# Channel weights of the first norm applied behind the transposes, in a one-core decoder layer

## The chip, the core and the metric

The kernel runs on one core of a Trainium2 chip. A core has a matrix engine (TensorE, PE in the profile), a vector engine (VectorE, DVE), a scalar engine (ScalarE, ACT), a small general engine (GpSimd, POOL), and queues from which transfers are started (SyncE, SP, carries nearly all of them here). The engines run on their own and wait for one another through semaphores. The metric is device time in microseconds (us) of one launch; lower is better.

## What is computed

One layer of a decoder trunk in float32: a norm, one wide input projection, three groups of heads (spatial gating, a gated delta rule, attention into 256 memory tokens), an output projection and a last norm. The change concerns the first norm and the norm of the memory tokens, each with a weight for every one of 2048 channels:

```python
def rmsnorm(x, g):
    xf = x.astype(jnp.float32)
    y = xf * lax.rsqrt(jnp.mean(xf * xf, axis=-1, keepdims=True) + EPS)
    return (y * g.astype(jnp.float32)).astype(x.dtype)

h = rmsnorm(x, ln_g[l])                      # x: 1024 x 2048
proj = h @ w_in[l]
...
m = rmsnorm(mem, mem_norm_g[l])              # mem: 256 x 2048
mk, mv = jnp.split(m @ w_mem_kv[l], 2, axis=-1)
```

## The kernel before

**Precision.** A float32 operand that has to be multiplied exactly enough is split into a high and a low part of the fast matmul type. `split_to` (L422) does this: ACT copies the source to the high part, DVE subtracts the high part from the source to get the low part. `triple` then issues three matmuls: high by high, high by low, low by high.

**Order.** Every instruction is recorded into a `Plan`. `Plan.issue` (L222) plays the recorded operations through a cost table (`price`, L181) and a priority (`rank`), engine by engine, and writes out the order that this gives. So all engines run a fixed program order that a planner chose when the kernel was built; a change of an operation's engine or of a buffer changes the order everywhere behind it. L277 is the one place from which all operations are issued, so every row of the profile has that line, and rows are told apart by their tiles.

**The first stage** (about the first 100 us) has three strands, which the planner interleaves:

- *Key and value weights.* The memory tokens are transposed and split (`spread_mem`, L521; tiles `gt` and `inv`). For each of 16 blocks `k` of 128 channels, `load_kv(k)` (L483) loads 128x1024 weights into a raw tile; ACT and DVE scale them by a column of the memory norm's weights (`gcol`, one column for each `k`) while splitting them into `whi` and `wlo`; PE accumulates 12 matmuls of 256 columns (keys, tiles `acc`) and 6 of 512 columns (values, the first two `dn` tiles). The raw tiles are a ring of four: two of `wraw`, two of `ut`. `kvmark` notes the last matmul of each `k`; some loads wait for such a mark.
- *The first norm's weights.* Each quarter of `ln_g` is loaded as one row into a `zg` tile. `spread_gain` (L532) spreads it over 128 partitions with a matmul against a row of ones, and ACT copies the result back. The four spread tiles are `gb`.
- *Tokens of x.* `prep(tt)` (L537) takes 128 tokens: sums of squares on ACT, a scale for each token from DVE and POOL, then for each quarter of the channels a DVE operation that multiplies by the token's scale and by `gb`, four PE transposes into a free bank (`spare()` hands out the last two `dn` banks in turn), and a hand-over `put`. For the first 512 tokens `put0` copies the bank to a `tn` tile on ACT, splits it into `ahi` and `alo`, and stores `tn` to `h0d`. For the other 512 tokens `prep1` runs later, beside the first projections, and `keep_rows` copies the bank to `tn` on ACT and stores it to `hTd`.

Behind the key and value matmuls PE starts on the projections: `project_first` (L871) goes over the first 256 tokens for all channels, then over the second 256. A quarter of channels of those tokens must be in `ahi` and `alo` before the matmuls on it. The weights of the projection come through the `wraw`, `whi` and `wlo` tiles in pieces of 512 columns of a row each (four blocks of 128 channels). In between come small preparations: a 105-row transpose of other weights (`y`), weights of the decay (`abw`), and weights of the spatial gating (tile `E`, transposed by PE, masked by DVE into `wsT`).

Of the kernel before, what the change touches and what calls it, by code (L numbers as in the profile page):

```python
# [12 lines left out]
ALU = mybir.AluOpType  # L13
# [4 lines left out]
P = 128  # L18
D = 2048
KT = D // P  # L20
NQ = 4
SEQ = 1024
HT = 512
# [39 lines left out]
class Plan:  # L63
# [21 lines left out]
    @contextmanager  # L85
    def rank(self, cls):
        old, self.cls = self.cls, cls
        yield
        self.cls = old
# [191 lines left out]
def kernel(  # L281
# [21 lines left out]
    x, mem, w_in, out = x[0], mem[0], w_in[0], out[0]  # L303
    w_mem_kv, w_out, conv_w = w_mem_kv[0], w_out[0], conv_w[0]
# [6 lines left out]
    V, S, G, PE, Q = R.dve, R.act, R.pool, R.pe, R.sp  # L311
    rank, behind = R.rank, R.behind

    def C(shape, name, dt=F32):
        return sb.tile(list(shape), dt, name=name, tag=name)[:]
# [38 lines left out]
    def bc(ap, n):  # L354
        return ap.unsqueeze(ap.ndim).to_broadcast(list(ap.shape) + [n])
# [4 lines left out]
    def tok(ap):  # L360

        return ap.rearrange("p (t c) -> p t c", c=P)
# [12 lines left out]
    kvraw = [*wraw.bufs]  # L375
# [5 lines left out]
    ring = {t: Slots(t, 4, [P, HT]) for t in ("kT", "qT", "vs", "kd", "ai")}  # L381
# [3 lines left out]
    zgb = ring["zg"].bufs  # L385
# [23 lines left out]
    ident, ones, utri = (C([P, P], n) for n in ("ident", "ones", "utri"))  # L409
# [12 lines left out]
    def split_to(hi, lo, src, eng):  # L422
        S.copy(hi, src)
        eng.tensor_tensor(out=lo, in0=src, in1=hi, op=ALU.subtract)
# [20 lines left out]
    def triple(a, l, r, start, stop, cls=9):  # L445

        mm(a, l[0], r[0], start, False, cls)
        mm(a, l[0], r[1], False, False, cls)
        return mm(a, l[1], r[0], False, stop, cls)
# [4 lines left out]
    def row_scale(xq):  # L454

        s = small()
        for c in range(4):
            S.activation(jk, xq[c], AF.Square, accum_out=s[:, c : c + 1])
        V.tensor_reduce(s[:, 4:5], s[:, 0:4], axis=AX.X, op=ALU.add)
        V.tensor_scalar(s[:, 4:5], s[:, 4:5], 1.0 / D, EPS, op0=ALU.mult, op1=ALU.add)  # L460
        rsqrt_to(s[:, 5:6], s[:, 4:5])
        return s[:, 5:6]


    def row_tiles(tag):
        if tag in ("inv", "gt", "ut"):
            return [b[:, i * HT : (i + 1) * HT] for b in (ring[tag](), ring[tag]()) for i in range(2)]
        return [ring[tag]() for _ in range(4)]

    gb = [ring["zg"]() for _ in range(4)]  # L470
    kvraw += [ring["ut"]() for _ in range(2)]
    mem_rows = [row_tiles("kT"), row_tiles("qT")]
    x_rows = {}

    def load_mem(q):
        for mt in range(2):
            Q.dma_start(mem_rows[mt][q], mem[mt * P : (mt + 1) * P, q * HT : (q + 1) * HT])

    def kv_parts(k):
        n = XW if k == 0 else 2 * XW  # L480
        return [slice(i, i + n) for i in range(0, 2 * XW, n)]

    def load_kv(k):  # L483
        for sl in kv_parts(k):
            Q.dma_start(kvraw[k % 4][:, sl], w_mem_kv[k * P : (k + 1) * P, sl])

    def load_x(tt, tag, after=(None,) * 4):
        x_rows[tt] = row_tiles(tag)
# [3 lines left out]

    y1 = C([P, 2 * NT, 32], "y1")
    rows = y1.rearrange("p c m -> p (c m)")[:, 0:P]
    mrow = rows[0:16]
    with rank(2):
        load_mem(0)
        S.dma_start(mrow, mem_norm_g[0].rearrange("(c p) -> c p", p=P))
        for c in range(4):
            S.dma_start(gb[c][0:1], ln_g[0:1, c * HT : (c + 1) * HT])  # L500
        for k in range(4):
            load_kv(k)
            if k == 1:
                load_mem(1)
    with rank(3):
        load_mem(2)
        load_mem(3)

    va, ka = dnr.bufs[0:2], acc
# [2 lines left out]
    def spare():  # L512
        turn["dn"] = 1 - turn["dn"]
        return flip[turn["dn"]]

    pt = spare()
    PE.transpose(pt[:, 0:16], mrow, ident[0:16, 0:16])
    gcol = C([P, 16], "gcol")
    with rank(1):
        V.tensor_copy(gcol, pt[:, 0:16])  # L520
    def spread_mem(q):  # L521
        h, l = (ring[t](F32R).rearrange("p (k n) -> p k n", k=4) for t in ("gt", "inv"))
        for mt in range(2):
            tp = spare()
            for k in range(4):
                PE.transpose(tp[:, k * P : (k + 1) * P], mem_rows[mt][q][:, k * P : (k + 1) * P], ident)
            sl = slice(mt * P, (mt + 1) * P)
            with rank(2):
                split_to(h[:, :, sl], l[:, :, sl], tok(tp), V)
        return h, l  # L530

    def spread_gain(c, pt):  # L532
        PE.matmul(pt, ones[0:1], gb[c][0:1], start=True, stop=True)
        with rank(3):
            S.copy(gb[c], pt)

    def prep(tt, put, bank):  # L537

        xq = x_rows[tt]
        r = row_scale(xq)  # L540
        for q in range(NQ):
            V.scalar_tensor_tensor(xq[q], xq[q], r, gb[q], op0=ALU.mult, op1=ALU.mult)
            tp = bank()
            for k in range(4):
                PE.transpose(tp[:, k * P : (k + 1) * P], xq[q][:, k * P : (k + 1) * P], ident)
            put(q, tok(tp))

    def keep_rows(dst, q, tt, tp):
        t = ring["tn"]()
        S.copy(t, tp.rearrange("p t c -> p (t c)"))  # L550
        Q.dma_start(dst[4 * q : 4 * q + 4, :, tt * P : (tt + 1) * P].rearrange("k p n -> p k n"), tok(t))

    def put0(tt):
        def put(q, tp):
            t = tok(ring["tn"]())
            with rank(1):
                S.copy(t, tp)
            with rank(2):
                split_to(ahq[q][:, tt], alq[q][:, tt], t, V)
            with rank(6):  # L560
                Q.dma_start(h0_d[4 * q : 4 * q + 4, :, tt * P : (tt + 1) * P].rearrange("k p n -> p k n"), t)

        return put
# [5 lines left out]
    mhl.append(spread_mem(1))  # L569
    for k in range(KT):  # L570
        mh, ml = mhl[k // 4]
        if k >= 4:
            with rank(3):
                load_kv(k)
        hi, lo = kvhi[k % 2], kvlo[k % 2]
        with rank(2):
            for sl in kv_parts(k):
                raw = kvraw[k % 4][:, sl]
                S.activation(hi[:, sl], raw, AF.Copy, scale=gcol[:, k : k + 1])
                V.scalar_tensor_tensor(lo[:, sl], raw, gcol[:, k : k + 1], hi[:, sl], op0=ALU.mult, op1=ALU.subtract)  # L580
        kk = k % 4
        for h in range(NX):
            sl = slice(h * P, (h + 1) * P)
            triple(ka[h][:, :NMEM], (hi[:, sl], lo[:, sl]), (mh[:, kk], ml[:, kk]), k == 0, k == KT - 1)
        for mt in range(2):
            sl = slice(mt * P, (mt + 1) * P)
            triple(va[mt], (mh[:, kk, sl], ml[:, kk, sl]), (hi[:, XW:], lo[:, XW:]), k == 0, k == KT - 1)
        kvmark.append(R.ops[-1])
        if 1 < k < 6:
            spread_gain(k - 2, spare())  # L590
        if k in (3, 7):
            mhl.append(spread_mem(k // 4 + 2))
        if k == 1:
            load_x(0, "vs", kvmark[1:2] * 4)
        if k == 4:
            load_x(1, "kd", kvmark[4:5] * 4)
        if k == 5:
            prep(0, put0(0), spare)
            for mt in range(2):
                rm.append(C([P, 1], f"rm{mt}"))  # L600
                V.tensor_copy(rm[mt], row_scale(mem_rows[mt]))
        if k == 7:

            dg, rmb = (ring["E"]()[:, 0:NMEM] for _ in range(2))
            for mt in range(2):
                V.tensor_scalar(dg[:, mt * P : (mt + 1) * P], ident, rm[mt], None, op0=ALU.mult)
            pt = spare()
            PE.matmul(pt[:, 0:NMEM], ones, dg, start=True, stop=True)
            S.copy(rmb, pt[:, 0:NMEM])
        if k == 9:  # L610
            prep(1, put0(1), spare)
            load_x(2, "kT", (kvmark[6], kvmark[7], kvmark[7], kvmark[8]))
        if k == 13:
            load_x(3, "qT", (kvmark[10], kvmark[11], kvmark[11], kvmark[12]))
            with rank(2):
                prep(2, put0(2), spare)
# [6 lines left out]
    for mt in range(2):  # L623
        t = [ring["ai"](F32R) for _ in range(2)]
# [9 lines left out]
    for h in range(NX):  # L634
        t = ring["vs"](F32R).rearrange("p (s m) -> p s m", s=2)
# [18 lines left out]
    pt = dnr()  # L654
# [30 lines left out]
    tp = dnr()  # L685
# [4 lines left out]
    tp = dnr()  # L690
    for g in range(NG):
        sl = slice(g * P, (g + 1) * P)
# [53 lines left out]
    def prep1(i):  # L746
        load_x(NT + i, "ut")
        prep(NT + i, lambda q, tp: keep_rows(hT_d, q, i, tp), over(scan_banks))
# [496 lines left out]
    ut = levels(state[2], *state[-1])  # L1245
# [313 lines left out]
    with rank(2.6):  # L1559
        for hf in range(2):  # L1560
            for p in range(NJ // 2, NJ):
                state = front_late(p, hf, late_inv[hf * 2 + p - NJ // 2])
                ut = levels(state[2], *state[-1])
# [38 lines left out]
    for n, (tag, to) in enumerate((("gt", mkT), ("inv", mv))):  # L1602
        for i in range(NX // 2):
            t = ring[tag](F32R).rearrange("p (h s m) -> p h s m", h=2, s=2)
# [190 lines left out]
```

## Time and profile before

| | us |
|---|---|
| device time, median of three runs | 1631.83 |
| lowest and highest of the three | 1628.95, 1632.06 |
| profiled execution, first to last instruction | 1631.6 |
| PE busy | 1613.6 (99%) |
| DVE busy | 1319.3 (81%) |
| ACT busy | 1025.9 (63%) |
| POOL busy | 114.7 (7%) |

The profiled execution has no other time than its span. A group row of the profile names the engine, the operation, the tile written and the tiles read, the shapes, the count, the busy time in us, the mean of one in ns, and then the idle time of the engine before such instructions. A timeline row gives start and duration in us and, in brackets, idle time before it and what ended that. A window row gives its stretch, its length, and the busy time of PE, PE's weight loads, DVE, ACT and POOL with their counts, then the granted PE clock, the DMA share and GB/s. Matmuls overlap in the records: a 512-column one is shown as 0.39 us, while the next starts 0.23 us after it.

### The profile page before, as it was taken

How to read it: one execution, taken by the hardware profiler on the slowest of the kernel's cores; microseconds unless marked ns; L12 is line 12 of the kernel's file. 1: busy time of each engine (PE TensorE's matmuls, PEld its weight loads, DVE VectorE, ACT ScalarE, POOL GpSimd, SP SyncE). 2: the span in 40 equal slices, each digit the busy share in tenths (PEclk: the TensorE clock that was granted, in tenths of full speed). 3: DMA queues.
4: the chain of work that ended last, by engine and by line, in shares of the span. 5: the costliest groups of instructions: out<-in, count | busy, mean ns of one | idle time of the engine just before them, and what ended most of it. 6: DMA issues, size and time to landing. Idle time of an engine off the chain costs nothing.

```text
span 1631.6 us, 25647 instructions
## 1 busy us (share of the span) xinstructions
PE 1613.6 (99%) x8570; PEld 1354.7 (83%) x8570; DVE 1319.3 (81%) x2288; ACT 1025.9 (63%) x2235; POOL 114.7 (7%) x139
## 2 busy tenths in 40 slices
PE   8999999999999999999999999999999999999997
PEld 6888888888888888888888888888888888888886
DVE  4876786858879869899999998888778897678875
ACT  5958674676755356877686547766657774344355
POOL 0100110020210000100101001001000000000001
PEclk9999999999999999999999999999999999999999
DMA  7888896886886867589867967889768889678646
GB/s 247 248 256 268 262 307 179 264 264 204 284 297 212 278 207 236 186 288 342 285 223 257 344 214 232 283 279 305 261 216 283 272 291 332 202 270 301 213 147 240
DMA packets 316846, 419.44 MB, mean 257 GB/s; under 512 B 51821, under 2 KB 140582, under 8 KB 316714
## 3 DMA queue, kind: packets, MB, share of 16 engines
q1 hardware_dynamic: 315010, 414.65, 77.8%
q0 software_dynamic: 1088, 2.10, 0.5%
q8 instruction: 67, 1.10, 0.3%
q10 hardware_dynamic: 616, 1.07, 0.2%
q14 instruction: 65, 0.53, 0.1%
HBM read 334.33 MB, written 82.87 MB: 256 GB/s over the span
## 4 chain that ended last, share of the span: by engine, by line
PE 95%; DMA 2%; DVE 2%; issue 1%; ACT 0%; POOL 0%; POOLq 0%; SPq 0%; DVEq 0%; ACTq 0%
PE acc L277 73%; PE dn L277 22%; DMA raws<-sd 1%; DMA kT<-in_mem_dram 1%; DVE wlo L277 1%; DVE alo L277 0%; DMA el<-vd 0%; DMA late<-kd 0%; DMA wraw<-in_w_in_dram 0%; DVE kT L277 0%; DVE kd L277 0%; ACT whi L277 0%; POOL small L277 0%; ACT jk L277 0%; DVE xr L277 0%
## 5 line engine op out<-in xcount | busy, mean ns | idle before, releaser
L277 PE MATMUL acc<-ahi,whi 128*128 128x512 f32 (+1 forms) x1152 | 451.4, 392 | 0.6 <-ACT whi L277 0.5
L277 PE MATMUL acc<-alo,whi 128*128 128x512 f32 (+1 forms) x1152 | 450.7, 392 | 0.0
L277 PE MATMUL acc<-ahi,wlo 128*128 128x512 f32 (+1 forms) x1152 | 450.0, 391 | 0.4 <-DVE wlo L277 0.4
L277 PEld LDWEIGHTS acc<-ahi,whi 128*128 128x128 f32 x1152 | 216.8, 188 | 42.0 <-ACT whi L277 1.0
L277 PEld LDWEIGHTS acc<-ahi,wlo 128*128 128x128 f32 x1152 | 216.8, 188 | 41.4 <-DVE wlo L277 0.6
L277 PEld LDWEIGHTS acc<-alo,whi 128*128 128x128 f32 x1152 | 216.9, 188 | 40.2
L277 PE MATMUL acc<-ahi,zh 128*128 128x512 f32 x736 | 233.6, 394 | 0.0
L277 ACT CAST whi<-wraw 128x512 fp32r<-128x512 f32 (+1 forms) x170 | 137.0, 807 | 102.3 <-PE acc L277 69.0
L277 ACT CAST ahi<-raws 128x1024 fp32r<-128x1024 f32 x131 | 137.4, 1049 | 84.0 <-PE acc L277 37.5
L277 DVE TENSOR_TENSOR alo<-raws,ahi 128x1024 fp32r<-128x1024 f32 x131 | 160.2, 1223 | 36.6 <-ACT ahi L277 36.0
L277 DVE TENSOR_TENSOR wlo<-wraw,whi 128x1024 fp32r<-128x1024 f32 (+1 forms) x138 | 134.5, 975 | 38.8 <-ACT whi L277 32.0
L277 PEld LDWEIGHTS acc<-ahi,zh 128*128 128x128 f32 x736 | 137.6, 188 | 27.1
L277 PE MATMUL acc<-ahi,zl 128*128 128x512 f32 x368 | 145.1, 394 | 0.0
L277 DVE TENSOR_TENSOR ahi<-y,ahi 128x1024 fp32r<-128x1024 f32 x65 | 79.3, 1220 | 21.3 <-ACT ahi L277 20.9
L277 ACT CAST ahi<-y 128x1024 fp32r<-128x1024 f32 x65 | 68.1, 1048 | 40.9 <-PE acc L277 23.0
L277 PEld LDWEIGHTS acc<-ahi,zl 128*128 128x128 f32 x368 | 69.3, 188 | 13.0
L277 ACT CAST zh<-wraw 128x1024 fp32r<-128x1024 f32 x36 | 37.8, 1049 | 43.8 <-PE acc L277 26.5
L277 POOL TENSOR_TENSOR hs<-hs,mhalf 128x4 f32<-128x4 f32 x32 | 48.0, 1502 | 234.3 <-DVE hs L277 223.8
L277 PE MATMUL dn<-whi,alo 128*128 128x512 f32 x152 | 59.0, 389 | 0.0
L277 PE MATMUL dn<-wlo,ahi 128*128 128x512 f32 x152 | 59.0, 389 | 0.0
L277 PE MATMUL dn<-whi,ahi 128*128 128x512 f32 x152 | 58.9, 389 | 0.0
L277 POOL TENSOR_TENSOR small<-small,mhalf 128x1 f32<-128x1 f32 x26 | 17.5, 677 | 581.5 <-DVE small L277 575.3
(408 smaller groups left out, 3210.4 us busy)
## 6 DMA issues: line engine op xcount, KB each, us to landing
wraw<-in_w_in_dram SPq DMA_DIRECT2D x86, 512.0 KB
raws<-sd SPq DMA_DIRECT2D x74, 512.0 KB
wraw<-in_w_in_dram SPq DMA_DIRECT2D x96, 256.0 KB
y<-in_w_in_dram SPq DMA_DIRECT2D x42, 512.0 KB
y<-sd SPq DMA_DIRECT2D x38, 512.0 KB
wraw<-in_w_out_dram SPq DMA_DIRECT2D x32, 512.0 KB
raws<-h0d SPq DMA_DIRECT2D x27, 512.0 KB
low<-wlo SPq DMA_DIRECT2D x32, 256.0 KB
```

Source lines behind the costliest of these rows:

```text
L277: o.fn(*o.args, **o.kw)
```

## The change

The rows of `ln_g` are no longer spread. They are loaded as 16 more rows beside those of the memory norm, and the one small transpose that makes `gcol` makes 32 columns instead of 16; `lcol` names the 16 new ones, four for each quarter. `prep` multiplies by the token's scale alone (`tensor_scalar` in place of `scalar_tensor_tensor`). Behind the transposes the channels lie on the partitions, and the copy from the bank to `tn`, which was ACT's, becomes a DVE multiplication by the column. This holds for `put0` and for `keep_rows`. `spread_gain`, its four matmuls and four ACT copies are gone. The two double tiles of `zg`, which `gb` held, join the ring of raw key and value weights: six instead of four, and the loads for `k` = 4 and 5 are issued between the third and the fourth quarter of the memory tokens.

```diff
-    gb = [ring["zg"]() for _ in range(4)]
-    kvraw += [ring["ut"]() for _ in range(2)]
+    kvraw += [ring["ut"]() for _ in range(2)] + zgb
+    NR = len(kvraw)
...
-            Q.dma_start(kvraw[k % 4][:, sl], w_mem_kv[k * P : (k + 1) * P, sl])
+            Q.dma_start(kvraw[k % NR][:, sl], w_mem_kv[k * P : (k + 1) * P, sl])
...
-    mrow = rows[0:16]
+    mrow = rows[0:32]
...
-        S.dma_start(mrow, mem_norm_g[0].rearrange("(c p) -> c p", p=P))
-        for c in range(4):
-            S.dma_start(gb[c][0:1], ln_g[0:1, c * HT : (c + 1) * HT])
+        S.dma_start(mrow[0:16], mem_norm_g[0].rearrange("(c p) -> c p", p=P))
+        S.dma_start(mrow[16:32], ln_g[0].rearrange("(c p) -> c p", p=P))
...
         load_mem(2)
+        for k in range(4, NR):
+            load_kv(k)
         load_mem(3)
...
-    PE.transpose(pt[:, 0:16], mrow, ident[0:16, 0:16])
-    gcol = C([P, 16], "gcol")
+    PE.transpose(pt[:, 0:32], mrow, ident[0:32, 0:32])
+    gcol = C([P, 32], "gcol")
...
+    lcol = [gcol[:, 16 + 4 * q : 20 + 4 * q] for q in range(NQ)]
...
-    def spread_gain(c, pt):
-        PE.matmul(pt, ones[0:1], gb[c][0:1], start=True, stop=True)
-        with rank(3):
-            S.copy(gb[c], pt)
...
-            V.scalar_tensor_tensor(xq[q], xq[q], r, gb[q], op0=ALU.mult, op1=ALU.mult)
+            V.tensor_scalar(xq[q], xq[q], r, None, op0=ALU.mult)
...
     def keep_rows(dst, q, tt, tp):
         t = ring["tn"]()
-        S.copy(t, tp.rearrange("p t c -> p (t c)"))
+        V.tensor_tensor(out=tok(t), in0=tp, in1=bc(lcol[q], P), op=ALU.mult)
...
             with rank(1):
-                S.copy(t, tp)
+                V.tensor_tensor(out=t, in0=tp, in1=bc(lcol[q], P), op=ALU.mult)
...
-        if k >= 4:
+        if k >= NR:
...
-                raw = kvraw[k % 4][:, sl]
+                raw = kvraw[k % NR][:, sl]
...
-        if 1 < k < 6:
-            spread_gain(k - 2, spare())
```

More of the change, by code (lines that the diff above doesn't have):

```diff
@@ L516 @@
     pt = spare()
-    PE.transpose(pt[:, 0:16], mrow, ident[0:16, 0:16])
-    gcol = C([P, 16], "gcol")
+    PE.transpose(pt[:, 0:32], mrow, ident[0:32, 0:32])
+    gcol = C([P, 32], "gcol")
     with rank(1):
-        V.tensor_copy(gcol, pt[:, 0:16])
+        V.tensor_copy(gcol, pt[:, 0:32])
+    lcol = [gcol[:, 16 + 4 * q : 20 + 4 * q] for q in range(NQ)]
     def spread_mem(q):
```

## Prediction

> **What bounds the kernel now.** I read the page first, for the engine that sets the end, then windows, to see where that engine has any idle time, then the timeline of PE and DVE in the stage that the change touches.
>
> ```profile
> span 1631.6 us, 25647 instructions
> PE 1613.6 (99%) x8570; PEld 1354.7 (83%) x8570; DVE 1319.3 (81%) x2288; ACT 1025.9 (63%) x2235; POOL 114.7 (7%) x139
> PE 95%; DMA 2%; DVE 2%; issue 1%; ACT 0%; POOL 0%; POOLq 0%; SPq 0%; DVEq 0%; ACTq 0%
> ```
>
> PE is busy 99% and makes 95% of the chain that ended last. Work taken from PE shortens the end one for one; work moved among ACT, DVE and DMA costs nothing until PE waits for it. In the windows the first figure behind the length is PE, the third DVE, the fourth ACT.
>
> ```profile
> 65.00:71.60 6.60, 6.42 (x44) 5.43 (x43) 6.60 (x12) 6.60 (x16) 0.23 (x1) 1.00 0.63 180
> 71.60:81.00 9.40, 8.46 (x68) 7.99 (x68) 8.96 (x18) 8.96 (x22) 1.52 (x1) 1.00 0.80 165
> 81.00:97.00 16.00, 16.00 (x92) 13.79 (x91) 9.63 (x22) 6.45 (x14) 0.00 (x0) 1.00 1.11 335
> 97.00:125.00 28.00, 28.00 (x151) 23.53 (x151) 22.50 (x60) 19.78 (x51) 2.33 (x4) 1.00 0.75 208
> 125.00:1600.00 1475.00, 1473.17 (x7784) 1235.21 (x7783) 1216.89 (x2093) 918.95 (x2017) 101.08 (x110) 1.00 0.79 258
> 600.00:700.00 100.00, 98.88 (x484) 83.08 (x483) 86.50 (x132) 74.85 (x171) 9.12 (x13) 1.00 0.63 202
> ```
>
> From 125 to 1600 us PE idles 1.8 us in all. From 65 to 81, where the key and value work ends and the first projection begins, it idles 0.18 + 0.94 = 1.12 us, and there DVE and ACT are both full. That is the place where work moved from ACT to DVE can reach PE.
>
> **The change part by part.** *The spreading goes.*
>
> ```profile
> L277 PE MATMUL dn<-zg,ones 1*128 1x512 f32 x8 | 4.0, 614 | 0.0
> L277 ACT COPY zg<-dn 128x512 f32<-128x512 f32 x4 | 2.3, 581 | 0.5 <-PE dn L277 0.5
> L277 ACT COPY tn<-dn 128x512 f32<-128x512 f32 x16 | 9.1, 588 | 0.7 <-PE dn L277 0.4
> ```
>
> Four matmuls (eight passes) leave PE: **−4.0 us**. ACT loses four copies of `zg` and 16 of `tn` in the stage, 11.4 us, but ACT is only a supplier.
>
> *The clock.* Three equal stretches of the key and value work:
>
> ```profile
> 15.00:18.40 3.40, 3.40 (x14) 1.75 (x13) 1.28 (x1) 2.21 (x3) 0.00 (x0) 1.00 0.94 374
> 18.40:21.90 3.50, 3.50 (x19) 3.42 (x18) 0.00 (x0) 0.00 (x0) 0.00 (x0) 0.51 0.60 189
> 21.90:25.30 3.40, 3.40 (x22) 3.04 (x21) 0.81 (x1) 1.15 (x1) 0.00 (x0) 1.00 0.83 256
> ...
> 30.00:45.00 15.00, 15.00 (x94) 12.29 (x93) 10.70 (x17) 14.30 (x29) 1.11 (x2) 1.00 0.81 263
> ...
> 15.76 1.98 PE L277 MATMUL dn<-zg,ones 1*128 1x512 f32 x4
> 30.89 1.98 PE L277 MATMUL dn<-zg,ones 1*128 1x512 f32 x4
> ```
>
> The granted clock falls to 0.51 in the stretch that follows the first pair of spreading matmuls, which fill 1.98 of its predecessor's 3.40 us with matmuls on one row. Without them the predecessor holds full matmuls. If that lifts the dip, half of 3.5 us is saved, 1.7; if the dip has another cause, nothing. The second pair, at 30.89, is followed by no such dip (1.00 from 30 to 45), so I take **−1.5 us**, bounds −1.7 and 0. [...]
>
> *The start.* In the changed program order PE's first matmul on values is followed at once by the transposes of the second memory quarter, which before came behind five more matmuls:
>
> ```profile
> 9.32 1.10 PE L277 MATMUL acc<-gt,whi 128*128 128x256 f32 x4
> 10.22 0.63 PE L277 MATMUL dn<-wlo,gt 128*128 128x512 f32 x1
> 11.01 1.12 PE L277 MATMUL dn<-ident,kT 128*128 128x128 f32 x4 [0.16 <-DMA kT<-in_mem_dram]
> ```
>
> Those transposes wait for a transfer until 11.01, and it is issued no earlier now. So the five matmuls from 9.32 to 10.85 are done later, while the wait is idle: between 0.6 us (done at the full clock) and 1.5; I take **+1.0**. Transposing 32 rows instead of 16, and one transfer in place of four, lie within the same wait: nothing.
>
> *The deeper ring.*
>
> ```profile
> L277 ACT ACTIVATE whi<-ut,gcol 128x1024 fp32r<-128x1024 f32 x8 | 9.2, 1151 | 6.8 <-PE dn L277 6.6
> 44.63 1.08 ACT L277 CAST gt<-dn 128x512 fp32r<-128x512 f32 x2
> ```
>
> Before their splits ACT waits 6.6 of 6.8 us for PE to free `whi`, so the raw weights were there in time: earlier loads gain nothing. The two added ones (1 MB, 2.8 us at the 374 GB/s above) go ahead of the fourth memory quarter, which is split at 44.63, some 30 us later: nothing; without that lead, up to 2.8.
>
> *DVE's load.*
>
> ```profile
> L277 DVE SCALAR_TENSOR_TENSOR vs<-vs,small,zg 128x512 f32<-128x512 f32 x4 | 2.8, 746 | 0.0
> L277 DVE TENSOR_SCALAR E<-E 128x512 f32<-128x512 f32 x1 | 0.4, 420 | 0.0
> L277 DVE TENSOR_TENSOR inv<-dn,gt 128x512 fp32r<-128x512 f32 x8 | 5.3, 687 | 9.3 <-ACT gt L277 9.3
> ...
> 68.32 1.27 DVE L277 SCALAR_TENSOR_TENSOR wlo<-ut,gcol,whi 128x1024 fp32r<-128x1024 f32 x1
> 69.52 0.68 DVE L277 TENSOR_TENSOR wlo<-wraw,whi 128x512 fp32r<-128x512 f32 x1
> 70.12 0.68 DVE L277 TENSOR_TENSOR alo<-tn,ahi 128x512 fp32r<-128x512 f32 x1
> 70.72 1.40 DVE L277 TENSOR_TENSOR xr<-acc,E 128x256 f32<-128x256 f32 x4
> 72.05 0.67 DVE L277 TENSOR_TENSOR alo<-tn,ahi 128x512 fp32r<-128x512 f32 x1
> ```
>
> Starts give the pace: 0.60 us for a 512-wide operation of two tensors, 0.33 for a 256-wide one. The new multiplication from the bank is like `inv<-dn,gt`: 0.60. The scaling that loses its second tensor lies between 0.42 (`E<-E`, one tensor, a constant) and the 0.746 that it replaces; it reads one tensor, so I take 0.40 at pace, against 0.66 before. For 128 tokens DVE gains 4 x 0.60 and loses 4 x 0.26: +1.36 us, 10.9 over eight.
>
> *What that does behind the key and value work.* Let T be the end of DVE's split for the last `k` (69.52 us before; PE sets the pace up to there, so T moves with it). PE's pace:
>
> ```profile
> 18.01 0.28 PE L277 MATMUL acc<-gt,wlo 128*128 128x256 f32 x1
> 18.13 0.28 PE L277 MATMUL acc<-gt,whi 128*128 128x256 f32 x1
> 22.13 0.40 PE L277 MATMUL dn<-whi,inv 128*128 128x512 f32 x1
> 22.36 0.39 PE L277 MATMUL dn<-whi,gt 128*128 128x512 f32 x1
> 59.19 0.60 PE L277 MATMUL dn<-ident,kd 128*128 128x128 f32 x4
> ```
>
> 0.12 us for 256 columns, 0.23 for 512, about 0.45 for a group of four transposes (its 0.60, less the 0.16 by which records overlap in the rows above). Before, the first two groups of 128 tokens were finished by T, and the last `alo` of the fourth was done at T + 14. In the changed order, DVE still has after T: the last quarter of the second group, multiplications and splits of the third, everything of the fourth, and the same pieces of projection weights. Following both queues:
> (a) The second piece of projection weights is split behind two new multiplications, a piece, four `xr`, two `alo` and two small ones: T + 5.3. PE has 2.2 us of key and value work and 12 matmuls, done at T + 3.6: waits 1.7.
> (b) Then four scalings, a multiplication and the third piece: T + 8.1. PE needs it at T + 7.4: waits 0.7.
> (c) Two splits, three more pieces' worth, two `ai`, a `vs` and the late quarter bring the second group's last `alo` at T + 14.2. PE has 10 narrow and 12 wide matmuls and three transpose groups: done at T + 13.4: waits 0.8.
> (d) PE next has 24 narrow and 8 wide matmuls and three transpose groups, done near T + 20.2; then it wants to transpose the fourth group's last quarter into a bank that DVE empties only behind constants, three `alo`, a piece and four `wsT`: T + 22.3. Waits 2.1. Ahead of `wsT` stands a load of `E` that SP issues behind the stores of `tn` and `kvd`, at T + 16; should it land after T + 20, (d) grows by that.
> Together 5.3 us, less the 1.1 idle before: **+4.2**. Bounds: 0, if the 11.4 us that ACT loses let DVE run ahead before T, and +7, if the scalings keep 0.66 and the `E` load is 1.5 late.
>
> *The second 512 tokens.* From 97 to 125 us DVE is busy 22.50 of 28 us and gains up to 5.4: hardly any slack, and PE's transposes now wait for DVE to empty their two banks, with piece splits in the same queue. **+1.0**, bounds 0 and 3.
>
> *The new order behind.* Almost every PE row behind 100 us stands elsewhere. PE idles 1.8 us there, so a new order can win no more; what it can lose has no such end. The worst 100 us (600 to 700) idle 1.12; half of the 14 such stretches like that would be 8. I take the middle of −1.8 and 8: **+3**.
>
> Sum: −4.0 − 1.5 + 1.0 + 4.2 + 1.0 + 3 = +3.7. The span is 1631.6 us, 0.2 below the median of the runs, so 1631.8 + 3.7 = **1635.5 us**. About 0.2% (3.3 us, the spread of the three runs) is what a measurement can tell from none.
>
> **The rivals.**
> *Faster: DVE keeps ahead.* T is early because ACT no longer holds the bank copies, and the last three terms vanish: −4.5, 1627.3 us. For it: ACT is full from 65 to 71.6 and its row above falls by 11.4 us. Against it: DVE is as full there and receives what ACT loses. It decides if the waits (a) to (d) stay below 1.2 us together.
> *The same: a draw.* The stage is as I work it out, but the new order costs nothing: +0.7, 1632.5 us. For it: PE is fed everywhere else in the profile. Against: the plan was made for other costs, with one scaling at the price of two tensors.
> *Clearly slower.* The scalings do not get quicker and the clock dip stays: +1.5 and +2.8 on the forecast, 1639.8 us. For it: only one row shows the quick form, with a constant; the dip is not repeated at 31 us. Against: `E<-E` has the same shape and memory.
>
> **How the numbers follow.** Forecast with the clearly slower case: 0.43 (the latter 0.10), its own range 1635.1 to 1643. A draw 0.28. Faster 0.29. For 8 in 10 the range runs from 1625, the faster case with some of the 1.8 us, to 1644, the clearly slower one with half of the order's 8. Faster than 1628.5: 0.29; within: 0.28; slower than 1635.1: 0.43.
>
> **What would show it.** No `dn<-zg` row and a granted clock near 1.00 from 18.4 to 21.9 (term two). PE idle until 11 us behind its first 512-wide matmul (three). `TENSOR_SCALAR` rows of 128x512 near 0.45 us and `tn<-dn,gcol` near 0.69 (four). Between 65 and 95 us, PE idle some 5 us with waits on DVE's `wlo`, `alo` and `tn`; if it stays near 1 us, the prediction is wrong and the faster case holds. Behind 125 us PE idle above 1.8 us shows the last term.

## The result, and the profile after

| | median us | range, runs | ratio to before |
|---|---|---|---|
| before | 1630.57 | 1628.95 to 1632.06, 4 | |
| after | 1651.73 | 1650.56 to 1653.74, 4 | 1.0128 [1.0115, 1.0140] |

The changed kernel is slower by 21 us. (A fourth run of the kernel before moves its median from 1631.83 to 1630.57.) 1635.5 us was forecast, within 1625 to 1644: the direction holds, the size doesn't. The page of the changed kernel:

```profile
span 1649.6 us, 25623 instructions
PE 1617.8 (98%) x8562; PEld 1356.0 (82%) x8562; DVE 1328.4 (81%) x2320; ACT 1008.5 (61%) x2199; POOL 103.6 (6%) x139
PE 92%; DVE 3%; DMA 1%; issue 1%; ACT 1%; SPq 0%; POOLq 0%; POOL 0%; DVEq 0%; ACTq 0%
```

PE has eight passes less and yet is busy 4.2 us longer (1617.8 against 1613.6), and the span of this one execution grew by 18.0 (the medians lie 21 apart). So there are two things to look for: idle time, and matmuls that take longer. Windows of the changed kernel (behind the length: PE, PEld, DVE, ACT and POOL busy, the granted clock, DMA share and GB/s) show where both are:

```profile
18.40:21.90 3.50, 3.50 (x25) 3.16 (x23) 1.34 (x2) 1.31 (x2) 0.00 (x0) 1.00 0.91 308
65.00:71.60 6.60, 5.05 (x39) 4.47 (x39) 6.34 (x14) 4.05 (x10) 0.55 (x1) 1.00 0.63 162
71.60:81.00 9.40, 8.84 (x59) 7.64 (x58) 8.84 (x23) 2.90 (x6) 0.00 (x0) 1.00 1.08 257
81.00:97.00 16.00, 10.82 (x61) 9.22 (x60) 7.98 (x16) 3.62 (x6) 0.00 (x0) 0.79 0.72 222
97.00:125.00 28.00, 28.00 (x141) 23.14 (x140) 18.33 (x49) 14.51 (x40) 0.55 (x1) 1.00 0.65 182
488.00:502.00 14.00, 9.13 (x47) 7.34 (x46) 11.57 (x31) 7.39 (x26) 0.20 (x1) 0.88 0.56 175
779.00:795.00 16.00, 12.53 (x50) 9.44 (x49) 11.01 (x23) 11.31 (x32) 1.61 (x2) 0.79 0.91 313
125.00:1600.00 1475.00, 1465.56 (x7728) 1226.46 (x7728) 1213.26 (x2094) 910.20 (x2007) 91.49 (x112) 1.00 0.80 256
```

The dip at 18.4 us is gone (1.00, before 0.51). From 65 to 97 PE idles 1.55 + 0.56 + 5.18 = 7.3 us, where before it was 1.1. From 125 to 1600 it idles 9.4 us, before 1.8, and nearly all of that lies in two places, 4.9 us at 488 and 3.5 us at 779. In all three places the granted clock falls too: 0.21 of 16 us, 0.12 of 14 us and 0.21 of 16 us come to 3.4, 1.7 and 3.4 us. The trace's clock records put the half clock at 85.70 to 92.53, 495.30 to 498.71 and 785.43 to 792.26 us; PE is busy for 4.53, 3.24 and 5.83 us of these, and half of that, 2.3, 1.6 and 2.9 us, is what its matmuls lose on top of the idle time. PE's timeline (start, length, and in brackets the idle time ahead with what ended it) at the three places, with the clock's mark at the last:

```profile
68.00 0.39 PE L277 MATMUL acc<-ahi,wlo 128*128 128x256 f32 x1 [1.48 <-DVE wlo L277]
76.86 0.39 PE L277 MATMUL acc<-alo,whi 128*128 128x256 f32 x1 [0.56 <-DVE alo L277]
83.77 0.66 PE L277 MATMUL dn<-ident,qT 128*128 128x128 f32 x4 [1.61 <-DVE tn L277]
86.43 1.11 PE L277 MATMUL dn<-ident,E 128*128 128x128 f32 x4 [2.00 <-DMA E<-in_gmlp_ws_dram]
89.11 1.12 PE L277 MATMUL dn<-ident,qT 128*128 128x128 f32 x4 [1.57 <-DVE tn L277]
489.12 0.60 PE L277 MATMUL dn<-steps,ut 128*128 128x128 f32 x4
491.08 0.71 PE L277 MATMUL dn<-steps,kd 128*128 128x128 f32 x4 [1.35 <-ACT steps L277]
...
493.58 1.07 PE L277 MATMUL dn<-states,kT 128*128 128x128 f32 x4 [0.90 <-ACT vs L277]
...
783.35 0.65 PE L277 MATMUL dn<-ident,kT 128*128 128x128 f32 x4 [1.24 <-ACT kd L277]
...
791.73 0.63 PE L277 MATMUL acc<-ahi,wlo 128*128 128x512 f32 x1
792.16 0.45 PE L277 MATMUL acc<-ahi,whi 128*128 128x512 f32 x1
792.45 0.39 PE L277 MATMUL acc<-alo,whi 128*128 128x512 f32 x1
792.68 0.40 PE L277 MATMUL acc<-ahi,wlo 128*128 128x512 f32 x1
```

At 489 us stand the steps of the recurrence, each of which needs what ACT or DVE makes of the one ahead. Between them stands no projection matmul. At 791.73 a 512-column matmul takes 0.43 us to the start of the next; from 792.45 the next starts after 0.23. The kernel before has the same steps of the recurrence at 471 us, with projections laid between them and no wait at all:

```profile
471.11 0.60 PE L277 MATMUL dn<-steps,ut 128*128 128x128 f32 x4
471.48 0.48 PE L277 MATMUL acc<-ahi,whi 128*128 128x512 f32 x1
...
472.93 0.61 PE L277 MATMUL dn<-steps,kd 128*128 128x128 f32 x4
```

To see where time goes over the whole span I use the lag: how much later than in the kernel before PE has streamed the same number of columns (worked out from all matmul records of both traces, the spreading left out of the count; a lag at 40 us is the one at the place that the kernel before reaches at 40 us). For the changed kernel it is −6.7 us at 40 us, +4.1 at 100, +2.5 at 480, +12.8 at 520, +13.4 at 760, +20.8 at 780 and +18.3 at the end.

### The profile page after: what moved, and what is told of

Its sections match the earlier page's. It is cut to its first block, busy times and chain, and to the rows that moved or that the text cites. A ratio compares the mean times of both kernels' runs of the same rounds, so it can differ in the third digit from the quotient of the medians.

```text
span 1649.6 us, 25623 instructions
## 1 busy us (share of the span) xinstructions
PE 1617.8 (98%) x8562; PEld 1356.0 (82%) x8562; DVE 1328.4 (81%) x2320; ACT 1008.5 (61%) x2199; POOL 103.6 (6%) x139
## 4 chain that ended last, share of the span: by engine, by line
PE 92%; DVE 3%; DMA 1%; issue 1%; ACT 1%; SPq 0%; POOLq 0%; POOL 0%; DVEq 0%; ACTq 0%
PE acc L277 71%; PE dn L277 21%; DVE wlo L277 1%; DVE y L277 0%; DMA xr<-pd 0%; DMA kT<-in_mem_dram 0%; ACT jk L277 0%; DMA wraw<-in_w_in_dram 0%; DVE alo L277 0%; DMA E<-in_gmlp_ws_dram 0%; DVE inv L277 0%; ACT whi L277 0%; DVE qT L277 0%; DVE ahi L277 0%; ACT ahi L277 0%
## 5 line engine op out<-in xcount | busy, mean ns | idle before, releaser
L277 ACT CAST ahi<-y 128x1024 fp32r<-128x1024 f32 x65 | 68.2, 1049 | 38.7 <-PE acc L277 19.7
L277 ACT CAST whi<-y 128x1024 fp32r<-128x1024 f32 x34 | 35.7, 1051 | 34.9 <-PE acc L277 25.7
```

The costliest lines, as they stand in the source:

```text
L277: o.fn(*o.args, **o.kw)
```

## The experiments

Two theories at first. Theory A: the planner, given other work, wrote another order, and the order costs the time. Theory B: the multiplications that DVE took over cost it, wherever they stand. The order can be taken apart from the work, because the planner's result is only a list of instructions. In three runs, and in all further ones that keep the order of before, the planner's choice is replaced by a given list:

```diff
     def issue(self):
-        free = dict.fromkeys(self.SEEN, 0.0)
...
-        self.ops.sort(key=lambda o: (o.at, o.idx))
+        seq = zlib.decompress(base64.b85decode(ORDER))
+        ops = []
+        for i in struct.unpack("<%dH" % (len(seq) // 2), seq):
+            ops += [self.ops[i], *self.ops[i].tail]
+        self.ops = ops
         for o in self.ops:
             o.fn(*o.args, **o.kw)
```

ORDER gives each instruction of one kernel the place of its counterpart in the other; what depends on a later one moves right behind it. Line numbers stay.

### Work and order apart

The changed work in the order of before:

> The changed kernel's instructions, issued in the order in which the kernel before issues its own (each instruction at the place of its counterpart; the spreading is gone). Theory A, the order: of the some 20 us lost, about 14 us (9.8 at 480 to 500 us and 7.5 at 760 to 790, less small gains) belong to the new order alone, so they vanish here; what is left is the gain of 6.7 us up to 45 us and what DVE's added work costs from 65 to 95 us, 4 to 11 us: 1628 to 1637 us, PE without holes near 490 and 785. Theory B, DVE's load: the multiplications that DVE took over cost the time in any order: 1645 to 1652 us.

Measured: 1632.36 us, ratio 1.0003 [0.9994, 1.0013]. The converse, the work of before in the changed order:

> The kernel before's instructions, issued in the order of the changed kernel (the four spreading matmuls stay, at their own places). Theory A, the order: the holes of PE near 490 and 785 us come with it although no work has moved: 1641 to 1652 us. Theory B, DVE's load: none of the added DVE work is there, so 1630 to 1635 us.

Measured: 1668.02 us, ratio 1.0218 [1.0199, 1.0238], even slower than the changed kernel, and more than either theory allowed.

| | order of before | order of the changed kernel |
|---|---|---|
| work of before | 1631.5 | 1668.0 |
| changed work | 1632.4 | 1651.7 |

The change of work alone costs nothing that can be told from zero; the order costs 19 us with the changed work and 36 with the old. The 36 is no price of an order in general: this order was made for other work, and 3.8 us of its lag stand already at 40 us, behind a start in which PE comes to its full pace only at 25 us. Theory B falls as the explanation of the 21 us. The waits of PE (total, times, longest) in the run with the old work and the changed order name the same places, without any new work on DVE:

```profile
PE dn L277 <- ACT tn L277: 3.5, 2, 2.0
PE dn L277 <- DMA E<-in_gmlp_ws_dram: 2.0, 1, 2.0
PE dn L277 <- ACT steps L277: 1.4, 1, 1.4
PE dn L277 <- ACT kd L277: 1.2, 1, 1.2
```

The holes at the recurrence (`steps`) and at 779 us (`kd`) came with the order. So did the `E` load, and at the end of the key and value work PE now waits for ACT's `tn` where it waited for DVE's. In the run with the changed work and the order of before, the stage and what lies behind it look so (windows, then PE's timeline):

```profile
65.00:71.60 6.60, 4.23 (x30) 3.54 (x29) 6.60 (x16) 5.11 (x12) 0.77 (x1) 1.00 0.66 170
71.60:81.00 9.40, 9.10 (x73) 8.38 (x72) 8.67 (x17) 5.08 (x13) 0.75 (x1) 1.00 0.93 243
```

```profile
67.69 0.36 PE L277 MATMUL acc<-ahi,whi 128*128 128x256 f32 x1 [1.23 <-DVE xr L277]
70.73 0.39 PE L277 MATMUL acc<-ahi,wlo 128*128 128x256 f32 x1 [1.14 <-DVE wlo L277]
...
1015.06 1.48 PE L277 MATMUL dn<-wsT,tn 128*128 128x128 f32 x8 [2.33 <-DMA tn<-vd]
```

DVE is full from 65 to 71.6 and PE waits for it; the clock stays at 1.00. The lag is −6.8 us at 40, −2.6 at 100, −2.2 at 1000, and +0.6 behind the wait for `tn` at 1015 us. So in a fixed order the new DVE work costs 4.2 us in the stage, and nothing more up to 1000 us. What makes the transfer at 1015 us late is not settled; the runs of the same order below don't wait there. Behind that wait PE is slow for some 3.4 us: the 512-column matmul at 1016.76 us takes 0.43 us to the start of the next, where ahead of the wait it took 0.23.

### The own order up to 95 us, the old one behind

> The changed kernel with its own order up to some 95 us and the order of the kernel before behind that. Theory A, the order: the loss at 65 to 95 us stays (about 11 us), the holes near 490 and 785 us go: 1634 to 1641 us. Theory B, DVE's load: 1648 to 1653 us, as the work is unchanged.

Measured: 1640.74 us, ratio 1.0059 [1.0044, 1.0074]. The lag is +6.1 us at 100 and between +7.8 and +9.1 from there on: no hole at 489 or 779. The part behind 95 us is worth 11 us; the remaining 9 are made ahead of 110 us.

### Other draws

If the order decides, changing a constant of the planner must move the time though no work changes. First, in the changed kernel:

```diff
-    SLACK = 600.0
+    SLACK = 580.0
```

> The changed kernel with one constant of its planner changed, the margin that PE's instructions are given, from 600 to 580 ns; no instruction is added, removed or moved to another engine. Theory A, the order: the time is that of another draw among orders, 1628 to 1643 us, and the holes stand elsewhere or not at all. Theory B, DVE's load: within 2 us of the changed kernel, 1650 to 1654 us.

Measured: 1638.88 us, ratio 1.0047 [1.0032, 1.0062]: 13 us less than the changed kernel with 600. Then in the kernel before:

```diff
-    DMA_FIXED = 1600.0
+    DMA_FIXED = 1700.0
```

> The kernel before with one constant of its planner changed, the fixed time of a transfer, from 1600 to 1700 ns; no instruction is added, removed or moved to another engine. Theory A, the order: its own order is one good draw, and another costs some 5 to 15 us without any change of the work: 1636 to 1647 us. Rival: the kernel before has room in every stage and a new order costs it nothing: 1630 to 1633 us.

Measured: 1656.47 us, ratio 1.0157 [1.0142, 1.0173]: 26 us for no change of work, more than theory A allowed. The longest of its waits, which the kernel before doesn't have:

```profile
PE acc L277 <- DVE y L277: 5.2, 1, 5.2
```

Perhaps the planner chose badly for a reason that can be mended: it prices a scaling of one tensor as one of two, and the scaling is new. The same edit in both kernels:

```diff
-            o.cost = (n + 151) / 0.96 + (60.0 if pointer and name == "scalar_tensor_tensor" else 0.0)
+            o.cost = 480.0 if name == "tensor_scalar" and n == HT else (n + 151) / 0.96 + (60.0 if pointer and name == "scalar_tensor_tensor" else 0.0)
```

> The changed kernel, with the planner's price of a one-tensor scaling of 512 columns set from 691 ns, at which it stands, to the 480 ns that the trace of the changed kernel shows for it (22 such instructions in the first 130 us, each 480 to 482 ns). No work changes. Theory A1, the wrong price: the plan thinks DVE fuller than it is and puts PE's work behind it; with the right price the holes at 81 to 97, 489 and 785 us go: 1626 to 1634 us. Theory A2, chance: any change of a price gives another draw, and this one is as likely bad as good: 1632 to 1648 us, around the 1638.9 of the run with the margin at 580 ns. Theory B, DVE's load: 1650 us; the runs so far speak against it.

Measured: 1643.08 us, ratio 1.0076 [1.0064, 1.0089].

> The same correction of the price in the kernel before, where 17 one-tensor instructions of 512 columns carry it, none of them in the first norm. It is the control: if the correction by itself makes better orders, this is faster than 1631.5 us by 2 us or more; if it matters only to the changed kernel's new scalings, 1630 to 1633 us; if any new plan is a new draw, 1631 to 1640 us.

Measured: 1631.05 us, ratio 1.0007 [0.9996, 1.0019]. The right price takes 9 us off the changed kernel, but leads to no good order: the lag is −1.0 us at 100 and rises to +9.0 at 400, where the changed kernel has no hole. Theory A1 missed; A2, chance, fits. The control says less than it should: in the kernel before, the price moved little. Set side by side by their tile names, PE's 8570 records of that trace differ from those of the kernel before in 105 lines, where the transfer constant makes 1903 and the change itself 2619.

### DVE's multiplications by themselves

In the order of before, the copies go back to ACT and the weights are left out:

```diff
-    V.tensor_tensor(out=tok(t), in0=tp, in1=bc(lcol[q], P), op=ALU.mult)
+    S.copy(t, tp.rearrange("p t c -> p (t c)"))
...
-                V.tensor_tensor(out=t, in0=tp, in1=bc(lcol[q], P), op=ALU.mult)
+                S.copy(t, tp)
```

> The changed kernel in the order of the kernel before, with the multiplication behind the transposes taken out again: ACT copies the bank as it did before, and the first norm's weights are left out of the result. Set against 1632.4 us with the multiplication. If DVE's multiplications cost the 4.2 us between 60 and 90 us that the trace of that run shows: 1627 to 1629 us, and DVE's waits at wlo, xr and tn there go. If those waits have another cause (the missing spreading lets PE run ahead of its suppliers): 1631 to 1633 us.

Measured: 1626.13 us, ratio 0.9974 [0.9965, 0.9984], 6.2 us less than with the multiplication, or 5.0 if each of the two is set against the kernel before on its own chip. The lag is −7.1 at 40 us and −7.3 at 100, with next to nothing of the waits for `wlo`, `xr` and `tn` that the changed work had in this order: 4.7 us are DVE's in the stage (−2.6 against −7.3), and the wait at 1015 us is absent too.

### The weights brought in by repeated rows

The gain can be had without new work on DVE. In the kernel before, in its own order:

```diff
-        for c in range(4):
-            S.dma_start(gb[c][0:1], ln_g[0:1, c * HT : (c + 1) * HT])
...
-    def spread_gain(c, pt):
-        PE.matmul(pt, ones[0:1], gb[c][0:1], start=True, stop=True)
+    def spread_gain(c):
         with rank(3):
-            S.copy(gb[c], pt)
+            Q.dma_start(gb[c], ln_g[0, c * HT : (c + 1) * HT].partition_broadcast(P))
```

> The kernel before in its own order, with the spreading taken out in another way: the four rows of weights come into their tiles by transfers that repeat one row over 128 partitions, so PE's four matmuls and ACT's four copies go, the scaling still multiplies by the weights, DVE gets nothing new, and the ring of raw weights stays at four tiles. The trace of the run without the multiplication stands 7.2 us ahead of the kernel before from 40 us on. If that gain is the spreading's and its clock's alone: 1622 to 1625 us, ahead of both kernels. If the deeper ring made part of it, or if the 1 MB of repeated rows holds up the raw weights: 1626 to 1632 us.

Measured: 1627.23 us, ratio 0.9968 [0.9957, 0.9978]: 4.4 us ahead of the kernel before on the same chip, and the fastest version here that computes the whole result. That lies in the second range, not in the first. Its profiled execution was the fastest of eight (1625.09 us), so the lag shows more than the median; by that lag, −6.5 us at 40 and at 100, the deeper ring made at most 0.6 of the 7.1 us in the run above. The same work with the planner's order:

> The work of the run with repeated rows, in the order that the planner makes for it. Theory A, the order: another draw, 1630 to 1655 us, though the work is some 7 us less than that of the kernel before. Rival: with no work moved to DVE the planner keeps what is gained: 1622 to 1627 us.

Measured: 1638.08 us, ratio 1.0040 [1.0026, 1.0053]. Even a pure saving loses to the order it is given: 10.9 us between the two orders.

### What the spreading did to the clock

The gain up to 40 us is larger than the 4.0 us of the spreading matmuls. To see whether their one row is the reason, the spreading was done on 128 rows:

```diff
+        for b in zgb:
+            G.memset(b, 0.0)
...
-        PE.matmul(pt, ones[0:1], gb[c][0:1], start=True, stop=True)
+        PE.matmul(pt, ones, gb[c], start=True, stop=True)
```

> The kernel before in its own order, with the spreading done on 128 rows instead of one (the weight tiles are set to zero first, and the ones have 128 rows; the result is the same). The streamed columns stay the same. If the clock falls after the spreading because its matmuls use one row of the array: granted 1.00 from 18.4 to 21.9 us, where the kernel before has 0.51, and 1.7 us less, 1628 to 1630 us. If the fall has another cause (four-pass matmuls as such, or an idle window at the start): 0.51 there again and 1630 to 1632 us.

Measured: 1636.94 us, ratio 1.0033 [1.0024, 1.0042]; neither time. The four loads of weights now waited on ACT's queue for the zeros, ACT's first work came at 12.6 us, and PE's lag at 10 us was +8.0. That it had shrunk to +3.5 by 40 us spoke for the clock, but a cleaner pair was needed, with the loads on SP's queue in both:

> The kernel before in its own order, with the four rows of weights loaded from SP's queue instead of ACT's; the spreading stays on one row. It is the reference for the next run. If ACT's first split then comes earlier and with it PE's start: up to 2 us less than 1631.6, 1629 to 1632 us; granted clock about 0.5 for one stretch of 3.4 us behind the first two spreading matmuls, as before.

Measured: 1632.64 us, ratio 1.0005 [0.9995, 1.0015].

> The same with the spreading on 128 rows (weight tiles set to zero first on POOL, ones of 128 rows; the same streamed columns, the same result), the weights loaded from SP's queue. If one-row matmuls count as idle for the clock: granted 1.00 throughout the first 45 us, 256-column matmuls at 0.12 us behind the spreading, and 1.7 us or a little more less than the run with one row. If the fall has another cause: the same dip in both, and the same time within 0.7 us.

Measured: 1629.99 us, ratio 0.9995 [0.9986, 1.0004]; 2.6 us less than with one row. The timeline and the windows behind the first spreading, one row:

```profile
15.18 1.98 PE L277 MATMUL dn<-zg,ones 1*128 1x512 f32 x4
...
17.72 0.42 PE L277 MATMUL acc<-gt,whi 128*128 128x256 f32 x1
17.93 0.41 PE L277 MATMUL acc<-inv,whi 128*128 128x256 f32 x1
```

```profile
15.00:18.40 3.40, 3.40 (x13) 1.98 (x11) 1.28 (x1) 2.21 (x3) 0.00 (x0) 0.84 0.77 287
18.40:21.90 3.50, 3.50 (x19) 3.37 (x19) 0.00 (x0) 0.00 (x0) 0.00 (x0) 0.67 0.79 215
```

And 128 rows:

```profile
15.21 1.96 PE L277 MATMUL dn<-zg,ones 128*128 128x512 f32 x4 [0.53 <-DMA zg<-in_ln_g_dram]
...
17.24 0.28 PE L277 MATMUL acc<-gt,wlo 128*128 128x256 f32 x1
17.36 0.28 PE L277 MATMUL acc<-gt,whi 128*128 128x256 f32 x1
```

```profile
15.00:18.40 3.40, 3.19 (x17) 2.26 (x17) 1.28 (x1) 2.09 (x3) 0.00 (x0) 1.00 0.90 312
18.40:21.90 3.50, 3.50 (x27) 3.24 (x26) 0.00 (x0) 0.96 (x1) 0.00 (x0) 1.00 0.80 239
```

The same 1.96 to 1.98 us of spreading, but behind one row the 256-column matmuls start 0.21 us apart and the clock falls to 0.84 and 0.67 in two windows (0.16 of 3.4 and 0.33 of 3.5, 1.7 us of work); behind 128 rows they start 0.12 apart at 1.00, although PE had idled 0.53 us ahead. In this pair the fall came with one row and not with 128; by the means of the 12 runs each the difference is 1.7 us (± 1.4, two standard errors), by the lag at 40 us 2.2. It is no fixed price of the spreading, though: in the run of the kernel before with the transfer constant the same one-row matmuls bring no fall, the clock is 1.00 in both windows and the 256-column matmuls start 0.12 us apart:

```profile
14.70 1.98 PE L277 MATMUL dn<-zg,ones 1*128 1x512 f32 x4
...
16.83 0.28 PE L277 MATMUL acc<-inv,whi 128*128 128x256 f32 x1
16.95 0.28 PE L277 MATMUL acc<-gt,wlo 128*128 128x256 f32 x1
```

What sets this run apart from the others is not shown.

## Why the prediction was wrong, point by point

*The spreading (−4.0) and the clock (−1.5, bounds −1.7 and 0)* stand. The second term is the difference of the runs with one row and 128 rows: 2.6 us by the medians, 1.7 by the means and by the granted clock. No idle time stands ahead of the fall in the kernel before: PE is busy through all of the 3.41 us of full clock from 15.03 to 18.44 us, 1.91 of them with the one-row matmuls (15.76 to 17.67). Why the second pair at 31 us brought no dip (1.00 from 28.7 to 45 us) no run shows. The lag of −6.5 to −7.1 us at 40 us in the order of before leaves about 1 us beyond the 5.7. It fits the time at which the full pace first comes: 15.0 us in the kernel before and 12.2 with the changed work in the same order, and half of the difference is 1.4 us. Whether the change or chance sets that time, one trace of each doesn't show.

*The start (+1.0).* At 20 us the changed kernel lags its work in the order of before by 0.7 us (−3.7 against −4.4), near the forecast, but the way there failed. PE was to idle until 11 us; the transposes come at 9.44, behind 0.53 us:

```profile
9.44 1.11 PE L277 MATMUL dn<-ident,kT 128*128 128x128 f32 x4 [0.53 <-DMA kT<-in_mem_dram]
```

The full pace comes 1.8 us later than in the other run (14.0 against 12.2 us), of which half, 0.9, would make the 0.7 by itself. The agreement is luck as far as the runs show.

*DVE's load behind the key and value work (+4.2).* The arithmetic of pieces is right: the scaling took 0.480 us, 0.40 at pace, and in the order of before the term measures 4.2 us by lag, 4.7 by taking the multiplications out. In the order that the kernel has, it measures 10.8 (−6.7 at 50 us to +4.1 at 100). Of the waits, (a) is 1.48 where 1.7 was forecast, (c) 0.56 for 0.8, (d) 1.57 and a second of its kind 1.61 for 2.1, (b) is absent; and the load of `E`, costed at nothing unless it landed late, holds PE for 2.00 us. That makes 7.2 for 5.3. What the step left out altogether is the clock behind such a cluster, 2.3 us more. Less the 1.1 idle before, that explains 8.4 of the 10.8; the rest isn't resolved. The old work in this order loses 10.0 between 80 and 90 us (+8.6 to +18.6), with ACT's `tn` in place of DVE's, so the excess goes with the order.

*The second 512 tokens (+1.0).* PE is busy 28.00 of 28 us there: 0.

*The new order behind (+3, bounds −1.8 and 8).* This is the step that failed. Its bound was "The worst 100 us (600 to 700) idle 1.12; half of the 14 such stretches like that would be 8", which takes the spread of one order for the spread of orders. The trace of before showed how well its own order fed PE and nothing of what another would do: the planner chooses step by step, and each of the five plans made here that order PE's work anew (1638.1, 1638.9, 1643.1, 1651.7 and 1656.5 us) is 6 to 26 us worse than the plan of before. That none is better suggests that the plan of before was a good draw and not a mean one; no run shows how it came about, or why the planner left the steps of the recurrence without projections here. In the changed kernel the term is 14.2 us by lag (4.1 to 18.3): 7.6 of idle time, 1.6 and 2.9 of clock, the rest not resolved.

The sum again, with measured terms: −6.7 up to 50 us, +10.8 to 100, +14.2 behind make +18.3, against 18.0 of span. The rival of a draw, "the new order costs nothing", is what the changed work gives in the order of before (1632.4 against a forecast of 1632.5); the order wasn't free. That the two figures agree is partly luck: by lag the gain up to 40 us was 6.8 where −4.0, −1.5 and +1.0 make 4.5, and the wait at 1015 us with its clock, which nobody forecast, took some 3 back.

## What to carry to other kernels

Where a program writes the order of all engines from estimated prices, a change of work has two costs: its own, which can be read from the stage, and a new order, which can't be read from the old trace. Hold the order fixed to measure the first, and try several orders before judging the change: here the work of the kernel before came to 1631 us in one planned order and to 1656 in another, and to 1668 in an order made for other work. A cluster of short PE waits should be costed with the clock that may fall behind it: in the changed kernel that was 2.3, 1.6 and 2.9 us more in three places.

## What the hardware showed beyond that

Matmuls on one row keep PE busy in the profile (1.98 us for a pair), and in two runs the clock came down to half behind them for one stretch of about 3.4 us; behind the same columns on 128 rows it stayed at 1.00. In the kernel before, the clock records of the trace have 1.00 from 15.03 to 18.44 us, 0.50 from there to 21.86 and 1.00 from there to 1626. The second pair, at 30.89 us, is followed by no fall, and with the transfer constant the first pair, at 14.70, isn't either. What decides it is not shown.

In the changed kernel the clock fell behind short waits, in three places where the longest is 2.00 us. Matmuls fill 0.66, 1.77 and 1.68 us of the 3.41 us ahead of 85.70, 495.30 and 785.43, and the half clock then lasts 6.83, 3.41 and 6.83 us. From 65 to 81 us of the same kernel, where PE is busy for 5.05 of 6.60 and 8.84 of 9.40 us, the clock stays at 1.00.

Last, these kernels start slow, and the windows don't say so. PE's timeline and a window of the run with the old work in the changed order, where the first two spreading matmuls stand 6 us apart, at 13.8 and 19.7:

```profile
19.69 2.07 PE L277 MATMUL dn<-zg,ones 1*128 1x512 f32 x2
...
23.78 0.41 PE L277 MATMUL acc<-gt,whi 128*128 128x256 f32 x1
23.99 0.41 PE L277 MATMUL acc<-inv,whi 128*128 128x256 f32 x1
...
25.26 0.28 PE L277 MATMUL acc<-gt,whi 128*128 128x256 f32 x1
25.38 0.28 PE L277 MATMUL acc<-inv,whi 128*128 128x256 f32 x1
```

```profile
18.40:21.90 3.50, 3.50 (x10) 1.77 (x9) 0.69 (x1) 0.59 (x2) 0.00 (x0) 1.00 0.02 7
```

Two passes of the spreading take 2.07 us where the prediction's row has 1.98 for four, and 256-column matmuls start 0.21 us apart up to 24 us and 0.12 from 25.26. The 1.00 of the window isn't a measurement of that time. In the kernel before, too, the first clock record stands at 15.03 us, and a window from 10.00 to 15.03, without any record, shows 1.00, though 256-column matmuls start 0.21 us apart there. Where records are missing, the pace of a known matmul is the witness.
